# Weight sums, couples and last products in a two-layer encoder trunk: a change of order on one core

## The chip, the cores and the metric

The kernel runs on one core of a Trainium2 chip. The metric is the device time of one execution in microseconds (us). Engines are named as in the profile: PE is TensorE (PEld its weight loads), DVE is VectorE, ACT is ScalarE, POOL is GpSimd, SP is SyncE, which here only issues DMAs. A line number such as L233 is a line of the kernel before; in the changed kernel the same code stands one to three lines further down.

## The reference

Two layers over 256 tokens of width 2048, all in float32. Each layer is a token mixer and a gated MLP with a convolution of width 3 over the tokens, both with RMSNorm ahead and the residual added.

```python
h = x
for layer in range(DEPTH):                         # DEPTH = 2
    hn = rmsnorm(h, norm_mix_g[layer])
    mix = mlstm_mixer(...) if layer % 2 == 0 else hgrn_mixer(...)
    h = h + mix
    h = h + conv_glu(rmsnorm(h, norm_ffn_g[layer]), ffn_w_up[layer], ..., ffn_w_down[layer])
return rmsnorm(h, final_g)

def conv_glu(hn, w_up, conv_w, conv_b, w_down):    # D_FF = 5504
    a, v = jnp.split(hn @ w_up, 2, axis=-1)
    c = conv_b + sum(ap[:, j:j + s] * conv_w[j] for j in range(3))   # ap: a, padded by one token
    return (jax.nn.gelu(c, approximate=False) * v) @ w_down
```

The first mixer is a bidirectional mLSTM (8 heads), the second a bidirectional HGRN2 (16 heads); each is a projection of the normalized tokens, a recurrence by head, and an output projection.

## The kernel before

**Products.** A float32 product is made of three products of rounded halves: a weight tile `raw` is rounded by ACT to `wh` (L145), and DVE takes the rest, `wl` = `raw` - `wh` (L146). The tokens are split likewise. Every product is high times high, high times low and low times high.

**Stages.** The program runs, for each layer: the mixer with its projections; then the MLP in two parts, of 22 and 21 tiles of 128 of the hidden width. A part is an *up half* (a chunk of matmuls for each tile: L343 and L347, then the convolution, GELU and product, which give the token tiles `g`) and a *down stage* of two *pairs*, which add the part's share of `w_down` to the residual `hm`, each for two of the four blocks of 512 columns. `squares_by_seven` writes a pair's matmuls (L233).

**Couples.** A pair works through *units* of two tiles of the hidden width: unit 0 is tiles 0 and 1, and so on to unit 10 (in the second part a single tile). Over two tiles, two token halves and two column blocks, a plain unit needs 8 block products (24 matmuls). A *couple* is a unit done by 7 block products (21 matmuls) in the manner of Strassen and Winograd: for it the weights' sums T1 to T4 and the token tiles' sums S1 to S4 are needed. `SEVEN[part]` lists which units are couples. Four of the products gather in the PSUM tiles `mm`, the rest in `pc` (C11, C12, C21, C22: first index the token half, second the column block).

**Weight sums ahead of time.** T1 to T4 are made earlier and kept in device memory (`tscr`): `prepare` loads a couple's weights into `praw` (two DMAs on SP), makes four subtractions on DVE (L608) and stores the result (two DMAs on SP, L611). In a down stage the couple then loads them back: three quarters into a tile `T` (L196), one quarter into the end of `raw` (L197). `T` shares its three buffers with `avc`, the temporaries of the up chunks. A list of sums (`todo`) is worked off at a fixed pitch beside the matmuls, counted on the kernel's own clock (`side`, advanced by what the matmuls are taken to last); there are three lists in each layer: one in the mixer (`prepare_early(mp, layer, first, period)`: first load at `first`, a sum each `period`), one in each up half (period `(nf * 10.4 - 26.0) / len(todo)`, each load asked for one sum ahead; in the mixers a load comes half a period ahead of its sum). `shares` and `SPLIT` say how many of a pair's sums go to the mixer, to the first and to the second up half.

**Order.** Instructions are written down as the code meets them, and a scheduler then reorders each engine's list by its own estimates; `pin` (`tc.keep_in_program_order`) holds instructions in the written order. Each engine then works strictly in its list's order.

**The end.** The last pair does its units 8, 9 and 10 in `ending`: all products of token half 0, then those of half 1; after each half, `FinalNorm.half` (L495 to L508) adds the two blocks to `hm`, takes the mean square, scales by it and sends the rows out. L495 adds the first block of a half, L497 the second, L507 scales.

Of the kernel before, what the change touches and what calls it, by code (L numbers as in the profile page):

```python
# [46 lines left out]
LEAD = 48  # L47
TEMP = 3
GATES = 4 * AH
SEVEN = (1, 2, 3, 4, 6, 7, 8, 9), (1, 2, 3, 4, 5, 6, 7)  # L50
SPLIT = (0, 2, 5), (2, 2, 3)
END = 3
SCRATCH = 4096
SEVEN_MIX = (2, 4, 6)
# [9 lines left out]
def trunk_kernel(ctx, tc, xT, x_d, fg_d, pp_d, cst_d, w_gate, w_first, w_aq, w_ak, w_av, w_ao, w_aout, w_ao2,  # L64
                 w_bq, w_bv, w_bg, w_bout, w_bo2, w_up, w_d0, w_d1, w_d3, out, mscr, tscr):
    nc = tc.nc
    act, dve, pool, pe = nc.scalar, nc.vector, nc.gpsimd, nc.tensor
# [60 lines left out]
    pin = tc.keep_in_program_order  # L128
# [94 lines left out]
    def squares_by_seven(ch, fetch, ready):  # L223

        P1, P6, P7, P5 = psm_ = banks() + banks()
        C11, C12, C21, C22 = psa_ = [aux("pc") for _ in range(4)]
        begun = set()
        held.append(ch)

        def product(ps, x, w, stop):  # L230
            (xh, xl), (wh, wl) = x, w
            for i, (a, b) in enumerate(((xh, wh), (xh, wl), (xl, wh))):
                pe.matmul(ps, a, b, start=id(ps) not in begun, stop=stop and i == 2)  # L233
                begun.add(id(ps))

        def half(x, t):
            return x[:, t * P:(t + 1) * P], x[:, T + t * P:T + (t + 1) * P]

        def block(p, i):
            return tuple(w[:, i * 512:(i + 1) * 512] for w in p)  # L240

        def ending(u0):
            while len(ready) < ch.nk - 2 * u0:
                fetch()
            for t in range(2):
                c, left = (C11, C12, C21, C22)[2 * t:2 * t + 2], iter(ready)
                for k in range(2 * u0, ch.nk, 2):
                    p = next(left)[:2]
                    x0, end = half(ch.x(k), t), k + 2 >= ch.nk
                    product(c[0], x0, block(p, 0), end)  # L250
                    if k + 1 == ch.nk:
                        product(c[1], x0, block(p, 1), end)
                        break
                    q, x1 = next(left)[:2], half(ch.x(k + 1), t)
                    product(c[1], x1, block(p, 1), False)
                    product(c[0], x1, block(q, 0), end)
                    product(c[1], x0, block(q, 1), end)
                ch.half(c, t)

        units, last = (ch.nk + 1) // 2, max(ch.seven)  # L260
        for u in range(units):
            if ch.last and u == units - END:
                ending(u)
                held.pop()
                return
            fetch()
            p = ready.pop(0)
            end = u == units - 1
            if 2 * u + 1 == ch.nk:
                x = ch.x(2 * u)  # L270
                for ps, t, w in ((C11, 0, 0), (C12, 0, 1), (C21, 1, 0), (C22, 1, 1)):
                    product(ps, half(x, t), block(p[:2], w), True)
                side.tick(2.7)
                break
            x0, x1 = ch.x(2 * u), ch.x(2 * u + 1)
            A11, A21, A12, A22 = half(x0, 0), half(x0, 1), half(x1, 0), half(x1, 1)

            def products(*them):
                for ps, x, w in them:
                    product(ps, x, w, u == last and ps in psm_)  # L280
                    side.tick(0.65)

            def piece():
                fetch()
                q = ready.pop(0)[:2]
                return block(q, 0), block(q, 1)

            B11, B22 = block(p[:2], 0), block(p[:2], 1)
            if u in ch.seven:
                S1, S3, S2, S4 = ch.sums(u)  # L290
                products((P1, A11, B11), (C12, S4, B22))
                T2, T3 = piece()
                products((P6, S2, T2), (P7, S3, T3))
                B21, T1 = piece()
                products((C11, A12, B21), (P5, S1, T1))
                T4, _ = piece()
                products((C21, A22, T4))
                if u == last:
                    ch.mid(psm_)
                    ch.rest = ch.ends  # L300
                continue
            B21, B12 = piece()
            for ps, (x, w), (y, v) in ((C11, (A11, B11), (A12, B21)), (C12, (A11, B12), (A12, B22)),
                                       (C21, (A21, B11), (A22, B21)), (C22, (A21, B12), (A22, B22))):
                product(ps, x, w, False)
                product(ps, y, v, end)
                side.tick(1.3)
        held.pop()
        ch.done(psa_)
# [309 lines left out]
    def prepare_early(mp, layer, first, period):  # L619
        todo, finished = early[layer]  # L620
        side.push(prepare(lambda i: [mp.tile([P, 1024], F32, tag=f"p{j}", name="praw") for j in range(2)],
                          todo, first, period, finished, late, False))
# [42 lines left out]
    def mlstm(norm, nxt):  # L665
# [8 lines left out]
        box = {}  # L674
# [182 lines left out]
        chunks = []  # L857
        for pr in range(AH // 2):
# [36 lines left out]
            def done_first(ps, done_v=done_v):  # L895
                pq = aux("pq")
                for k in range(KT):
                    o = k % 4 * GATES
                    pin(pe.matmul(pq[o:o + GATES, 0:T], gw[:, k], hx[:, k], start=k < 4, stop=k >= KT - 4))
                gs = ev.tile([P, T], F32, tag="gs", name="gs")  # L900
                act.copy(gs, pq[:, 0:T])
                startup.close()
                begin()
                norm.finish()
                done_v(ps, note)
                side.push(start(gs))
                prepare_early(box["mp"], 0, 45.0, 19.0)

            last = {}

# [32 lines left out]
    def hgrn(norm, nxt):  # L943
        YT = [None] * KT
        stack = ExitStack()
        box = {}

        def begin():
            mp = box["mp"] = stack.enter_context(tc.tile_pool(name="hg", bufs=1))
            late(cst[:, C_LV:], cst_d[:, C_LV:])  # L950
            prepare_early(mp, 1, 30.0, 26.0)
            box["turn"] = 0
            lb = box["lb"] = mp.tile([P, KT], F32, name="lb")
            oml = box["oml"] = mp.tile([P, KT], F32, name="oml")
            t0 = mp.tile([P, 2, KT], F32, name="t0")
            t1 = mp.tile([P, KT], F32, name="t1")
            raw = pp[:, OFF["lb"]:OFF["lb"] + 2 * KT].rearrange("p (a b) -> p a b", a=2)
            dve.tensor_tensor(t1, raw[:, 0], raw[:, 1], ALU.max)
            for i in range(2):
                dve.tensor_tensor(t0[:, i], raw[:, i], t1, ALU.subtract)  # L960
            act.activation(t0, t0, AF.Exp)
            dve.tensor_tensor(t1, t0[:, 0], t0[:, 1], ALU.add)
            dve.reciprocal(t1, t1)
            for i in range(2):
                dve.tensor_tensor(t0[:, i], t0[:, i], t1, ALU.mult)
            dve.tensor_tensor(lb, t0[:, 0], t0[:, 1], ALU.add)
            dve.tensor_tensor(lb, lb, t0[:, 0], ALU.subtract)
            dve.tensor_scalar(oml, lb, -1.0, 1.0, ALU.mult, ALU.add)
# [137 lines left out]
        chunks, vs, gs, fs = [], [], [], []  # L1106
        for qd in range(BH // 4):
# [16 lines left out]
            for i in range(6):  # L1124
# [4 lines left out]
                n = 6 * qd + i  # L1129
# [3 lines left out]
        for n, ch in enumerate(fs):  # L1133
            if n in TMS:
                i = TMS.index(n)
# [11 lines left out]
    def ffn(layer, norm, nxt):  # L1147
        stack = ExitStack()
        ending = isinstance(nxt, FinalNorm)
        box = {}  # L1150
        chunks, pairs, lists = [], [], []
# [36 lines left out]
        for part, (f0, nf) in enumerate(((0, FA), (FA, FB))):  # L1188
            GT, SX, todo, finished = [], {}, [], []
# [13 lines left out]
            def two(src, c0, norm, seven, shares, GT=GT, SX=SX, nf=nf):  # L1203
                ch = pair(src, nf, c0, lambda k: GT[k], lambda u: SX[u], norm, seven)
                ch.waits, left = [], list(seven)
                for n, (todo, finished) in zip(shares, [early[layer]] + lists):
                    for u in left[:n]:
                        store(ch, src, u, todo)
                    if n:
                        ch.waits.append(finished)  # L1210
                    left = left[n:]
                assert not left
                pairs.append(ch)
                return ch

            w0, w1 = w_d0[layer][:, f0 * 1024:(f0 + nf) * 1024], w_d3[layer] if part else w_d1[layer]
            n = len(SEVEN[part])
            chunks.append(two(w0, 0, nxt if part else None, SEVEN[part], (0, 0, n) if part else (n, 0)))
            chunks.append(two(w1, 2, nxt if part and not ending else None, SEVEN[part], SPLIT[layer] if part else (0, n)))
            if part:  # L1220
                chunks[-1].last = ending
# [12 lines left out]
    for i in range(90):  # L1234
        o = i % 4 * QUAD
# [3 lines left out]
    chunks = mlstm(n0, n1)  # L1239
    c, close0 = ffn(0, n1, n2)  # L1240
    chunks += c
    c = hgrn(n2, n3)
    b = c[0].before
# [6 lines left out]
    c, close1 = ffn(1, n3, nf)  # L1250
# [102 lines left out]
```

## Time and profile before

| | |
|---|---|
| time, median of 3 runs | 2377.87 us (2377.03 to 2379.53) |
| profiled execution, its own time | 2380.58 us |
| its span, first to last instruction | 2378.3 us |
| busy PE, DVE, ACT, POOL | 99%, 83%, 61%, 9% of the span |
| DMA | 632.96 MB, mean 266 GB/s |
| weight sums loaded back (`T<-tscr`) | 63 |
| first mixer, MLP, second mixer, MLP | to about 390, 1090, 1675, 2378 us |

A row of the timeline gives the start in us from the span's start, the duration, the engine, the line, the operation, what is written and read, and how many were merged into the row; in brackets stands the idle time of the engine before it and what ended that. A row of the waits gives total, number and longest. A row of the windows gives the stretch and its length, then busy time and number of instructions for PE, PEld, DVE, ACT and POOL (or of one engine, if a line is picked out), the granted clock (1.00 is full), the share of the DMA engines and their GB/s.

### The profile page before, as it was taken

The numbers are of one execution on the slowest core, as the hardware profiler recorded it, in microseconds if no ns is written. First come the engines' busy times: TensorE is split into PE (matmuls) and PEld (weight loads), VectorE is DVE, ScalarE is ACT, GpSimd is POOL, SyncE is SP. The second block draws the span as 40 slices with busy tenths as digits, with TensorE's granted clock in tenths as the row PEclk, the third lists the DMA queues.
The fourth block names the chain that finished last, engine by engine and source line by source line (L and its number), as shares of the span: only waits on it lengthen the run. The fifth ranks groups of instructions, "written<-read, shape, count | busy, mean of one in ns | idle before, by whom it ended". The sixth has DMA issues, their size and how long they took to land.

```text
span 2378.3 us, 38347 instructions
## 1 busy us (share of the span) xinstructions
PE 2360.9 (99%) x14548; PEld 2019.2 (85%) x14548; DVE 1965.4 (83%) x3028; ACT 1459.1 (61%) x2321; POOL 203.9 (9%) x244
## 2 busy tenths in 40 slices
PE   9999999999999999999999999999999999999998
PEld 8888888888888888888888888888888888888886
DVE  7777687888888898887888878878788878888887
ACT  7655456555565555675777676776555566455565
POOL 0100000000000000000332322220000000000000
PEclk9999999999999999999999999999999999999999
DMA  8787655887898888986666666656778798888895
GB/s 300 240 273 266 229 186 198 301 284 266 280 345 289 308 282 291 362 295 230 244 219 245 227 225 229 218 172 232 265 263 282 273 329 306 296 272 287 287 357 188
DMA packets 121832, 632.96 MB, mean 266 GB/s; under 512 B 13728, under 2 KB 14240, under 8 KB 77232
## 3 DMA queue, kind: packets, MB, share of 16 engines
q1 hardware_dynamic: 119952, 626.51, 75.1%
q0 software_dynamic: 1120, 3.21, 0.8%
q8 instruction: 114, 1.87, 0.3%
q10 hardware_dynamic: 576, 0.79, 0.1%
q14 instruction: 70, 0.57, 0.1%
HBM read 562.24 MB, written 68.22 MB: 265 GB/s over the span
## 4 chain that ended last, share of the span: by engine, by line
PE 94%; DMA 3%; DVE 2%; issue 1%; ACT 0%; SPq 0%; POOL 0%; DVEq 0%; POOLq 0%; ACTq 0%
PE mm L343 36%; PE mm L347 18%; PE mm L359 16%; PE pc L233 13%; PE mm L233 7%; DMA T<-tscr 1%; DMA praw<-in_w_d 1%; DVE wl L146 1%; PE pn L822 1%; PE py L1080 1%; PE pd L1030 0%; PE pz L420 0%; PE pa L1030 0%; DMA Mb<-mscr 0%; ACT wh L145 0%
## 5 line engine op out<-in xcount | busy, mean ns | idle before, releaser
L343 PE MATMUL mm<-xt,wh 128*128 128x512 f32 x3776 | 1312.8, 394 | 0.7 <-issue 0.7
L146 DVE TENSOR_TENSOR wl<-raw,wh 128x1024 fp32r<-128x1024 f32 (+1 forms) x844 | 1035.9, 1233 | 267.1 <-ACT wh L145 257.3
L145 ACT CAST wh<-raw 128x1024 fp32r<-128x1024 f32 (+1 forms) x844 | 875.1, 1043 | 544.5 <-PE mm L343 326.9
L347 PE MATMUL mm<-xt,wl 128*128 128x256 f32 x3776 | 1043.4, 278 | 0.0
L343 PEld LDWEIGHTS mm<-xt,wh 128*128 128x128 f32 x3776 | 705.5, 188 | 161.1 <-issue 0.8
L347 PEld LDWEIGHTS mm<-xt,wl 128*128 128x128 f32 x3776 | 709.4, 188 | 5.2 <-issue 0.4
L359 PE MATMUL mm<-wh,xt 128*128 128x512 f32 x1024 | 322.8, 393 | 1.1 <-ACT xt L365 1.0
L233 PE MATMUL pc<-wh,g 128*128 128x512 f32 x776 | 262.8, 390 | 0.0
L359 PEld LDWEIGHTS mm<-wh,xt 128*128 128x128 f32 x1024 | 191.3, 188 | 40.6 <-ACT xt L365 1.4
L359 PE MATMUL mm<-wl,xt 128*128 128x512 f32 x512 | 198.1, 391 | 0.0
L608 DVE TENSOR_TENSOR praw<-praw 128x512 f32<-128x512 f32 x252 | 174.5, 692 | 26.4 <-DMA praw<-in_w_d 21.7
L233 PEld LDWEIGHTS pc<-wh,g 128*128 128x128 f32 x776 | 145.6, 188 | 30.2
L233 PE MATMUL pc<-wl,g 128*128 128x512 f32 x388 | 150.9, 389 | 0.0
L233 PE MATMUL mm<-wh,sx 128*128 128x512 f32 x396 | 141.6, 390 | 1.0 <-ACT wh L145 1.0
L146 DVE TENSOR_TENSOR wl<-T,wh 128x1024 fp32r<-128x1024 f32 (+1 forms) x132 | 125.8, 965 | 16.4 <-ACT wh L145 16.2
L145 ACT CAST wh<-T 128x1024 fp32r<-128x1024 f32 (+1 forms) x132 | 109.4, 835 | 46.4 <-PE pc L233 19.9
L567 POOL TENSOR_TENSOR hm<-hm,u 128x512 f32<-128x512 f32 x10 | 13.9, 1389 | 1225.5 <-DVE u L566 1225.5
L1167 ACT COPY avc<-mm 128x256 f32<-128x256 f32 x172 | 64.1, 373 | 79.3 <-PE mm L347 79.1
L1043 DVE TENSOR_TENSOR QK<-QK,G 128x256 f32<-128x256 f32 x224 | 106.8, 525 | 6.8 <-ACT kq L1022 6.2
L359 PEld LDWEIGHTS mm<-wl,xt 128*128 128x128 f32 x512 | 96.2, 188 | 18.7
L1022 ACT COPY kq<-QK 128x512 f32<-128x512 f32 x112 | 74.2, 668 | 46.0 <-DVE QK L1043 41.3
L233 PEld LDWEIGHTS mm<-wh,sx 128*128 128x128 f32 x396 | 74.2, 188 | 17.1 <-ACT wh L145 1.8
(237 smaller groups left out, 2225.0 us busy)
## 6 DMA issues: line engine op xcount, KB each, us to landing
raw<-in_w_up SPq DMA_DIRECT2D x172, 1024.0 KB, 5.5
tscr<-praw SPq DMA_DIRECT2D x126, 512.0 KB, 6.8
praw<-in_w_d SPq DMA_DIRECT2D x120, 512.0 KB, 6.6
raw<-in_w_bq SPq DMA_DIRECT2D x48, 1024.0 KB, 5.0
T<-tscr SPq DMA_DIRECT2D x63, 768.0 KB, 7.1
raw<-in_w_d SPq DMA_DIRECT2D x60, 768.0 KB, 6.2
raw<-in_w_ao SPq DMA_DIRECT2D x24, 1024.0 KB, 4.9
raw<-in_w_d SPq DMA_DIRECT2D x24, 1024.0 KB, 6.2
```

What stands on the lines that cost most here:

```text
L145: pin(act.copy(wh[:, :m], r))
L146: pin(dve.tensor_tensor(wl[:, :m], r, wh[:, :m].bitcast(F32), ALU.subtract))
L233: pe.matmul(ps, a, b, start=id(ps) not in begun, stop=stop and i == 2)
L343: pe.matmul(ps[f], wh[:, c:c + P], x, start=k + kk == 0, stop=False)
L347: pe.matmul(ps[f][:, 0:T], wl[:, c:c + P], x[:, 0:T], start=False, stop=k + kk == ch.nk - 1)
L359: pe.matmul(ps[t], x[:, a + t * P:a + (t + 1) * P], w[:, c], start=st and i == 0, stop=sp and i == 2)
L608: dve.tensor_tensor(out, x, y, ALU.subtract)
L822: pe.matmul(pn[:, 0:258], w, v, start=(i == 0), stop=(i == len(parts) - 1))
L1022: act.copy(m, blocks(QK, h))
L1043: dve.tensor_tensor(two[:, j], two[:, j], by[:, j], ALU.mult)
L1080: pe.matmul(py[:, c], AT[:, s if s == t else 2 + s], V[:, s, j * P:(j + 1) * P], start=(s == 0), stop=(s == 1))
L1167: act.copy(z, p[:, T:2 * T])
```

## The change

It changes four things. The last pair's 60 products are held in the written order, and those of token half 1 are written with all of column block 0 ahead of column block 1. In the first part of each MLP the couples stand at units 2 to 9 (before: 1 to 4 and 6 to 9). The first pair of that part takes six of its eight sums from the mixer and two from the first up half (before: all eight from the mixer); the second layer's last pair takes none from its mixer (before: two). So the mixers make 6 and 9 sums (before: 8 and 13), and each of the four up halves makes 12 (before: 10 and 12 in layer 0, 10 and 10 in layer 1). Lastly `prepare_early` starts the mixers' sums at 62 with a pitch of 25, and at 30 with a pitch of 38 (before: 45 and 19, 30 and 26). The count of couples, of sums (63) and of matmuls is the same.

```diff
-SEVEN = (1, 2, 3, 4, 6, 7, 8, 9), (1, 2, 3, 4, 5, 6, 7)
-SPLIT = (0, 2, 5), (2, 2, 3)
+SEVEN = (2, 3, 4, 5, 6, 7, 8, 9), (1, 2, 3, 4, 5, 6, 7)
+FIRST = 6
+SPLIT = (0, 2, 5), (0, 2, 5)
...
-        def product(ps, x, w, stop):
+        def product(ps, x, w, stop, pin=lambda ins: ins):
             (xh, xl), (wh, wl) = x, w
             for i, (a, b) in enumerate(((xh, wh), (xh, wl), (xl, wh))):
-                pe.matmul(ps, a, b, start=id(ps) not in begun, stop=stop and i == 2)
+                pin(pe.matmul(ps, a, b, start=id(ps) not in begun, stop=stop and i == 2))
...
             for t in range(2):
-                c, left = (C11, C12, C21, C22)[2 * t:2 * t + 2], iter(ready)
+                c, todo, left = (C11, C12, C21, C22)[2 * t:2 * t + 2], [], iter(ready)
                 for k in range(2 * u0, ch.nk, 2):
-                    p = next(left)[:2]
-                    x0, end = half(ch.x(k), t), k + 2 >= ch.nk
-                    product(c[0], x0, block(p, 0), end)
+                    p, x0 = next(left)[:2], half(ch.x(k), t)
+                    todo += [(0, x0, block(p, 0))]
                     if k + 1 == ch.nk:
-                        product(c[1], x0, block(p, 1), end)
+                        todo += [(1, x0, block(p, 1))]
                         break
                     q, x1 = next(left)[:2], half(ch.x(k + 1), t)
-                    product(c[1], x1, block(p, 1), False)
-                    product(c[0], x1, block(q, 0), end)
-                    product(c[1], x0, block(q, 1), end)
+                    todo += [(1, x1, block(p, 1)), (0, x1, block(q, 0)), (1, x0, block(q, 1))]
+                if t:
+                    todo.sort(key=lambda o: o[0])
+                end = [max(i for i, o in enumerate(todo) if o[0] == j) for j in range(2)]
+                for i, (j, x, w) in enumerate(todo):
+                    product(c[j], x, w, i == end[j], pin)
                 ch.half(c, t)
...
-                prepare_early(box["mp"], 0, 45.0, 19.0)
+                prepare_early(box["mp"], 0, 62.0, 25.0)
...
-            prepare_early(mp, 1, 30.0, 26.0)
+            prepare_early(mp, 1, 30.0, 38.0)
...
-            chunks.append(two(w0, 0, nxt if part else None, SEVEN[part], (0, 0, n) if part else (n, 0)))
+            chunks.append(two(w0, 0, nxt if part else None, SEVEN[part], (0, 0, n) if part else (FIRST, n - FIRST)))
```

What becomes of the order shows at three places.

**PE, the last products of the program.** `pc_23407` and `pc_23408` are the two column blocks of token half 0, `pc_23409` and `pc_23410` those of half 1; g16 to g20 are the token tiles. Before, the last rows but the very end:

```order
L233 MATMUL pc_23407<-wh_23762,g20_22952 128x512
L233 MATMUL pc_23408<-wh_23762,g20_22952 128x512
L233 MATMUL pc_23408<-wl_23763,g20_22952 128x512
L233 MATMUL pc_23408<-wh_23762,g20_22952 128x512
L233 MATMUL pc_23409<-wh_23756,g19_22843 128x512
L233 MATMUL pc_23409<-wl_23757,g19_22843 128x512
L233 MATMUL pc_23409<-wh_23756,g19_22843 128x512
L233 MATMUL pc_23410<-wh_23756,g18_22733 128x512
```

After these, 8 more rows follow there: two of `pc_23410`, three of `pc_23409`, three of `pc_23410`. The scheduler had mixed the halves: half 0 ends 12 matmuls before the end, and the two blocks of half 1 end three matmuls apart. Now:

```order
L234 MATMUL pc_23408<-wl_23763,g20_22952 128x512
L234 MATMUL pc_23408<-wh_23762,g20_22952 128x512
L234 MATMUL pc_23409<-wh_23717,g16_22513 128x512
L234 MATMUL pc_23409<-wl_23718,g16_22513 128x512
L234 MATMUL pc_23409<-wh_23717,g16_22513 128x512
L234 MATMUL pc_23409<-wh_23727,g17_22621 128x512
```

Half 0 ends 30 matmuls before the end; 15 of `pc_23409` follow, and then 15 of `pc_23410`.

**DVE, the first two heads of the first mixer.** `W`, `Wl`, `rd` and `y` belong to the heads, `praw` to the weight sums. Before:

```order
L608 TENSOR_TENSOR praw<-praw 128x512
L797 SCALAR_TENSOR_TENSOR W<-Mb,cc,cst 128x256
L797 SCALAR_TENSOR_TENSOR W<-Mb,cc,cst 128x128 x2
L797 SCALAR_TENSOR_TENSOR W<-Mb,cc,cst 128x256
L146 TENSOR_TENSOR wl<-raw,wh 128x1024
L825 TENSOR_TENSOR rd<-rd,emn 128x1
L608 TENSOR_TENSOR praw<-praw 128x512
L825 TENSOR_TENSOR rd<-rd,emn 128x1 x3
L826 RECIPROCAL rd<-rd 128x1
L608 TENSOR_TENSOR praw<-praw 128x512
```

And now, from the same place on:

```order
L800 SCALAR_TENSOR_TENSOR W<-Mb,cc,cst 128x256
L800 SCALAR_TENSOR_TENSOR W<-Mb,cc,cst 128x128 x2
L800 SCALAR_TENSOR_TENSOR W<-Mb,cc,cst 128x256
L147 TENSOR_TENSOR wl<-raw,wh 128x1024
L828 TENSOR_TENSOR rd<-rd,emn 128x1 x4
L829 RECIPROCAL rd<-rd 128x1 x4
L147 TENSOR_TENSOR wl<-raw,wh 128x1024
L833 SCALAR_TENSOR_TENSOR y<-pn,rd,y 128x256 x2
```

The first sum (L611 in the new numbering) now comes 18 rows later, behind the last `y` of the first two heads.

**SP, the start of the first down stage.** `raw<-in_w_d` of 128x2048 is a plain unit, of 128x1536 a couple; `T` and `raw<-tscr` are its stored sums. Before:

```order
L133 DMA raw<-in_w_d 128x2048
L611 DMA tscr<-praw 128x1024 x2
L133 DMA raw<-in_w_d 128x1536
L197 DMA raw<-tscr 128x512
L133 DMA raw<-in_w_d 128x1536
L196 DMA T<-tscr 128x1536
L197 DMA raw<-tscr 128x512
```

And now:

```order
L134 DMA raw<-in_w_d 128x2048 x2
L614 DMA tscr<-praw 128x1024 x2
L134 DMA raw<-in_w_d 128x1536
L198 DMA raw<-tscr 128x512
L134 DMA raw<-in_w_d 128x1536
L198 DMA raw<-tscr 128x512
L197 DMA T<-tscr 128x1536
```

Two plain units stand ahead of the first couple instead of one, so the first T is that of unit 2.

## The prediction

> **What bounds the kernel now.** I read the page first: the busy shares, then the chain that ended last.
>
> ```profile
> PE 2360.9 (99%) x14548; PEld 2019.2 (85%) x14548; DVE 1965.4 (83%) x3028; ACT 1459.1 (61%) x2321; POOL 203.9 (9%) x244
> PE 94%; DMA 3%; DVE 2%; issue 1%; ACT 0%; SPq 0%; POOL 0%; DVEq 0%; POOLq 0%; ACTq 0%
> ```
>
> TensorE is the bound, and the change leaves its work alone: the same 13,313 matmuls of the same shapes stand in both programs (eight couples by seven before and after, only at other units). So the change can only give back time in which PE stands still, or add such time. Who keeps PE waiting is in the view of waits:
>
> ```profile
> PE pd L1030 <- issue: 1.1, 1, 1.1
> PE mm L233 <- ACT wh L145: 1.0, 2, 0.6
> PE pz L1101 <- DVE y L1095: 0.8, 1, 0.8
> PE mm L343 <- issue: 0.7, 1, 0.7
> PE pn L822 <- DVE y L830: 0.7, 1, 0.7
> PE pc L233 <- DVE wl L146: 0.3, 1, 0.3
> ```
>
> That is 4.6 us in 2378, besides the start of the program. The other time without matmuls is the end, after the last of them. 0.2% of the median of 2377.87 us is 4.8 us, about what a measurement of this kernel can tell from no change; so nearly all of this would have to go for a gain that shows. A matmul's shown end runs past the next one's start (0.39 us each, every 0.227 us below), so I size stalls by starts.
>
> **The end.** The timeline of the last microseconds:
>
> ```profile
> 2354.17 8.84 PE pc L233 x39
> 2367.15 0.62 PE L233 MATMUL pc<-wh,g 128*128 128x512 f32 x2
> 2367.83 0.39 PE L233 MATMUL pc<-wh,g 128*128 128x512 f32 x1
> 2367.65 0.69 DVE L495 TENSOR_TENSOR hm<-hm,pc 128x512 f32<-128x512 f32 x1 [0.31 <-PE pc L233]
> 2368.25 1.41 DVE L507 SCALAR_TENSOR_TENSOR hm<-hm,fss,fg 128x512 f32<-128x512 f32 x2
> 2369.58 0.68 DVE L497 TENSOR_TENSOR hm<-hm,pc 128x512 f32<-128x512 f32 x1
> 2371.92 1.42 DVE L507 SCALAR_TENSOR_TENSOR hm<-hm,fss,fg 128x512 f32<-128x512 f32 x2 [0.67 <-POOL fss L502]
> ```
>
> PE is done at 2367.83 + 0.39 = 2368.22, but the add that needs the last block (L497) starts at 2369.58: DVE first scales the first token half (L507, twice), which the old order ended late. By the new order the first token half ends 30 matmuls before the end, 6.8 us at 0.227 (8.84/39), and the block of L495 15 matmuls, 3.4 us, before it. The first half's adds then start near 2361.4 and its scaling near 2364.5 (an add of 0.7 and then 2.34, as from L497 to the last L507 now), L495 near 2364.9; all DVE work but the last block's is over by about 2367. L497 then starts 0.11 us after PE's end, as L495 does now behind the matmul of 2367.15 (end 2367.54, start 2367.65): 2368.33. The rest (L497 to scaling, 2.34 us, and the output DMAs) stays: **1.25 us saved**. Less contention among the output DMAs could add some tenths.
>
> The held order has a price if weights come late: PE may no longer take another half's product. The 60 products start at about 2367.83 − 59 × 0.227 = 2354.4.
>
> ```profile
> 2353.71 1.23 DVE L146 TENSOR_TENSOR wl<-raw,wh 128x1024 fp32r<-128x1024 f32 x1 [0.67 <-ACT wh L145]
> 2356.64 2.35 DVE L146 TENSOR_TENSOR wl<-raw,wh 128x1024 fp32r<-128x1024 f32 x2
> ```
>
> The last three pieces are split by 2354.9, 2357.8 and 2359.0. The held order takes their low parts as products 13, 19 and 25 (counted from 0): at 2357.4, 2358.8 and 2360.1. So the cover is 0.9 us at its thinnest; if these pieces come 2 us later, PE loses 1.1 and most of the gain is gone. I count nothing.
>
> **Couples at units 2 to 9.** At the start of a down stage the first couples wait for their stored sums, whose tiles are those of the last up chunks:
>
> ```profile
> 637.50 0.39 PE L233 MATMUL pc<-wh,g 128*128 128x512 f32 x1
> 641.00 6.31 SPq L196 DMA_DIRECT2D T<-tscr  x3
> 647.60 1.05 ACT L145 CAST wh<-T 128x1024 fp32r<-128x1024 f32 x1 [1.93 <-DMA T<-tscr]
> 647.96 0.39 PE L233 MATMUL pc<-wh,g 128*128 128x512 f32 x1
> 648.70 0.73 PE L233 MATMUL mm<-wh,sx 128*128 128x512 f32 x2 [0.35 <-ACT wh L145]
> 1930.71 0.39 PE L233 MATMUL pc<-wh,g 128*128 128x512 f32 x1
> 1931.71 0.50 PE L233 MATMUL mm<-wh,sx 128*128 128x512 f32 x1 [0.62 <-ACT wh L145]
> ```
>
> Unit 0 (24 matmuls, 5.4 us) and unit 1 (21, 4.8 us) pass; then unit 2 waits for a sum that was asked for at 641.00. The stalls are 0.74 − 0.23 = 0.51 and 1.00 − 0.23 = 0.77 us. With units 0 and 1 plain, that second sum belongs to unit 3 and is needed at 637.5 + 2 × 5.4 + 4.8 = 653.1 or later, 4.5 us after its cast is through at 648.65. **1.25 us saved** in the two layers, between 0.5 (one of them stays, for tiles freed later) and 1.3. What is late next is nothing that I see: two plain units ask less of all engines.
>
> The cost is that couples now stand eight in a row. Each asks for a stored tile T of 768 KB and, by the code's shapes (128x1536 and 128x512), for 768 and 256 KB in `raw`: 1.835 MB in 21 × 0.227 = 4.77 us, 385 GB/s. The page's row of T, and windows inside such rows of couples:
>
> ```profile
> T<-tscr SPq DMA_DIRECT2D x63, 768.0 KB, 7.1
> 665.00:670.00 5.00, 5.00 (x24) 4.14 (x23) 3.24 (x4) 2.62 (x4) 0.00 (x0) 1.00 1.02 418
> 685.00:690.00 5.00, 5.00 (x24) 4.14 (x23) 5.00 (x7) 4.01 (x4) 0.00 (x0) 1.00 0.97 361
> 1010.00:1015.00 5.00, 5.00 (x24) 4.14 (x23) 4.32 (x5) 3.93 (x5) 0.00 (x0) 1.00 1.01 417
> ```
>
> In the windows the last column is GB/s, the one before it the DMA engines' share. The last lies late in a row of seven couples (units 1 to 7, 985 to 1018), at 417 and with PE full: the DMA keeps up. I take 0. [...]
>
> **Sums moved.** A sum is four subtractions on DVE (L608) and four DMAs on SP, two in and two out. The mixers lose two of eight and four of thirteen; the first up half of each layer goes from ten to twelve, as does the second of layer 1. The windows of L608 alone, then of all engines, for a half with ten sums, one with twelve, and the second mixer:
>
> ```profile
> 392.00:640.00 248.00, 27.35 (x40) 1.00 0.81 277
> 757.00:980.00 223.00, 32.88 (x48) 1.00 0.88 306
> 392.00:640.00 248.00, 248.00 (x1432) 216.85 (x1431) 209.07 (x337) 141.07 (x223) 0.70 (x1) 1.00 0.81 277
> 757.00:980.00 223.00, 223.00 (x1289) 194.95 (x1288) 195.71 (x312) 125.50 (x197) 0.00 (x0) 1.00 0.88 306
> 1100.00:1605.00 505.00, 502.24 (x4613) 431.84 (x4612) 412.30 (x687) 354.41 (x679) 143.35 (x176) 1.00 0.65 225
> ```
>
> Two more sums are 8 × 0.684 (27.35/40) = 5.5 us of DVE: 209 to 215 of 248, 87%. The half with twelve runs at 88%, with PE full for all 223 us. So the twelve **cost 0**, PE's matmuls hiding them; their DMAs on SP as well, beside the loads of `raw`.
>
> In the mixers a sum's load isn't asked for a sum ahead, so DVE, which works in order, waits at L608 and holds up what PE needs:
>
> ```profile
> DMA to landing us min/median/max: 2.6/6.6/10.1
> 86.26 0.69 DVE L608 TENSOR_TENSOR praw<-praw 128x512 f32<-128x512 f32 x1 [1.82 <-DMA praw<-in_w_d]
> 92.37 0.28 PE L822 MATMUL pn<-Vh,Wl 128*128 128x258 f32 x1
> 93.32 0.39 PE L822 MATMUL pn<-Vh,Wh 128*128 128x258 f32 x1 [0.67 <-DVE y L830]
> 1373.15 0.69 DVE L608 TENSOR_TENSOR praw<-praw 128x512 f32<-128x512 f32 x1 [2.21 <-DMA praw<-in_w_d]
> 1385.41 0.39 PE L359 MATMUL mm<-wh,xt 128*128 128x512 f32 x1
> 1386.63 0.66 PE L1101 MATMUL pz<-cst,y 128*128 128x128 f32 x2 [0.84 <-DVE y L1095]
> ```
>
> The first sum of the first mixer stood among the work of the first two heads; it now stands behind it, so 1.8 us of waiting and 4 × 0.68 of work leave DVE there, and the stall of 0.95 − 0.12 = **0.8 us** goes. In the second mixer the load has half the pitch to land, 19 of the kernel's own units rather than 13, so fewer of DVE's waits should last; but sums fall beside other heads. Of the 1.22 − 0.23 = 1.0 us there I count **half, 0.5**: between 0 (another head pays) and 1.0. New stalls of this kind: between 0 and one more of 1.0; I take 0.2, since one sum in thirteen made one.
>
> **The sum.** 1.25 + 1.25 + 0.8 + 0.5 − 0.2 = 3.6 us. The profiled execution took 2380.58 us (2.3 beyond its span of 2378.3), so its like would take 2377.0; that execution lies 2.7 above the median of the runs, so I put the gain there: 2377.87 − 3.6 = **2374.3 us**.
>
> **The rivals.**
> *All stalls go (faster).* The two waits on "issue" (1.1 and 0.7 in the table; by name nothing that the profile shows) may be tied to the mixers' load, and DVE there may be free enough for the whole 1.0: 3.6 + 0.5 + 0.2 + 1.8, with 0.3 at the output, is 6.4: 2371.5. For it: both lie in the second mixer, which loses four sums. Against: nothing names their cause, and the order of small matmuls there shifts anyway.
>
> *The mixers' waits only move.* The end and the couples give 2.5, but each mixer keeps a stall, one of 1.3 beyond now: 2376.7. For it: one slip in order anywhere in 500 us is enough, as at 1385. Against: fewer sums, longer leads.
>
> *The eight in a row starve (slower).* If the supply sits where the row of 685 has it, 361 GB/s at a share of 0.97, a couple needs 5.08 us, 0.31 more than PE; four rows of eight cost 10 us once the loaded-ahead tiles are used up, and 2384.3 results. It decides when the mean supply over a row falls below 385. [...] Against: seven in a row at 417, without a stall.
>
> *Not what it says:* the order might not hold at the end; it is written as held, so I see no room for this.
>
> **How the numbers follow.** Forecast 0.44 (own range 2373.2 to 2375.6), waits moved 0.20, all go 0.28, starving 0.08. Faster by over 0.2% (below 2373.1) is the third alone, 0.28; slower by over 0.2% (above 2382.6) the fourth, 0.08; within, 0.64. The range of 8 in 10 takes in the forecast, the moved waits and most of the faster case, and stops short of starving: 2370.8 to 2378.0.
>
> **What would show it.** Right: L497's counterpart starts within 0.2 us of PE's last end; no wait of `mm` on `wh` in the first units of a down stage; the stall at 92 gone; PE full in all four up halves. Wrong: idle PE before `pc` in the last 14 us (weights late in the held order), waits of ACT on DMA late in units 5 to 9, new waits of PE on `y` or `W` in the mixers, or a wait on `praw` that stops PE in an up half.

## The result, and the profile after

| | before | after |
|---|---|---|
| median in the same comparison | 2379.54 us (2377.03 to 2381.53, 10 runs) | 2371.99 us (2370.0 to 2376.66, 10 runs) |
| ratio | | 0.9973, 95% interval 0.9963 to 0.9982 |
| profiled execution, its span | 2380.58, 2378.3 us | 2372.06, 2370.1 us |

Faster by 0.27%, some 6.4 us by that ratio (the medians lie 7.55 us apart). The forecast was 2374.3, with 3.6 us saved; the measured time lies inside the range, but beyond the forecast's own band (2373.2 to 2375.6) and close to the rival by which all stalls go (2371.5). The page of the changed kernel, its busy times:

```profile
PE 2357.5 (99%) x14548; PEld 2019.1 (85%) x14548; DVE 1965.9 (83%) x3028; ACT 1464.1 (62%) x2321; POOL 196.9 (8%) x244
T<-tscr SPq DMA_DIRECT2D x63, 768.0 KB, 8.1
```

The work is the same: as many instructions on PE, DVE and ACT. The waits, PE's rows but that of its first instruction, and the two of DVE on the loads of sums:

```profile
PE mm L346 <- issue: 1.5, 1, 1.5
PE mm L362 <- ACT xt L368: 0.6, 1, 0.6
PE pc L234 <- DVE wl L147: 0.4, 1, 0.4
...
DVE praw L611 <- DMA praw<-in_w_d: 26.0, 18, 3.5
DVE praw L611 <- issue: 17.1, 14, 2.2
```

PE's 4.6 us of waits have become 1.9; the row on `xt` lies at 9.7, in the start, which the 4.6 leave out (it is 1.0 there before). Those on `wh`, on `y` (both mixers) and on `pd` are gone; the longest left is one on "issue", at a place that had none before. DVE waits longer for `praw` (before: 21.7 us on the DMA), and the span is 8.2 us shorter all the same.

**By stage.** The following table is worked out from the trace: I cut the program where PE has done the same number of matmuls and compare the stages' lengths, by the matmuls' starts. The first row is the profiled execution of before; the others are differences to it (us). "End" is from PE's last start to the span's end. Stages that are left out differ by 0.03 at most (in e10 by 0.13), and the start of the program varies (-1.4 to +1.9, in one run +4.4). A row is one execution and need not be the typical one: those of e2 and e9 are the fastest of their kernels' runs, those of e1, e3 and e7 the slowest.

```
                       mixer 1  down 0a  up 0b  mixer 2  down 1a  up 1b  last down    end    span
before                  362.59   122.54 219.90   495.62   120.17 222.90     104.50  10.50  2378.3
after                    -1.97    -0.65   0.00    -2.83    -1.29   0.00       0.11  -1.33  2370.1
after, once more         -2.17    -0.65   0.00    -4.39    -1.29   0.00       4.23  -1.33  2371.5
e1  end alone             0.43     0.57   0.00     0.21    -1.29   0.00       0.00  -1.33  2376.8
e2  couples alone        -0.06    -0.65   0.00    -0.93    -1.29   0.00       0.03  -0.02  2374.1
e3  sums alone           -2.04    -0.49   0.00    -2.33     0.15   0.00       0.98  -0.21  2376.2
e4  old start and pitch  -0.37    -0.65   0.00    -2.28    -1.29   0.00       1.07  -1.31  2373.2
e5  sorted, not held     -1.75    -0.65   0.00    -2.27    -1.29   0.00       0.61  -0.35  2371.2
e6  held, not sorted     -1.93    -0.65   0.00    -2.79    -1.29   0.00       0.00  -1.19  2370.0
e7  122 for 90           -2.09    -0.65   0.00    -2.81    -1.29   0.00       1.84  -1.32  2376.4
e8  sums from 62 on      -1.93     0.61   0.00     1.30     0.25   0.00       0.30  -0.01  2377.6
e9  half ends 10 early   -2.09    -0.65   2.48    -3.15    -1.29   3.25       0.03  -1.33  2374.3
e10 loads asked earlier   5.59     0.12   0.00     1.57    -0.83   0.00       0.30  -0.01  2384.1
e12 74 for 90            -2.07    -0.65   0.00    -3.15    -1.29   0.00       0.31  -1.32  2370.0
```

Down 0a and 1a are the first parts' down stages, with the moved couples; up 0b and 1b the second up halves. After: 0.26 at the start, 1.97, 0.65, 2.83 and 1.29, less 0.11, and 1.33 are the 8.2 us of span.

**The end**, on the timeline after; its counterpart is the first one shown of before:

```profile
2358.03 0.69 DVE L498 TENSOR_TENSOR hm<-hm,pc 128x512 f32<-128x512 f32 x1 [1.02 <-PE pc L234]
2358.63 1.41 DVE L510 SCALAR_TENSOR_TENSOR hm<-hm,fss,fg 128x512 f32<-128x512 f32 x2
...
2360.93 0.39 PE L234 MATMUL pc<-wh,g 128*128 128x512 f32 x1
2361.36 0.69 DVE L500 TENSOR_TENSOR hm<-hm,pc 128x512 f32<-128x512 f32 x1 [1.19 <-PE pc L234]
2363.70 1.41 DVE L510 SCALAR_TENSOR_TENSOR hm<-hm,fss,fg 128x512 f32<-128x512 f32 x2 [0.67 <-POOL fss L505]
```

The add of the last block (L500, before L497) follows PE's last end, 2361.32, by 0.04 us; before, by 1.36. DVE has scaled the first half before that and waits 1.19 us for PE. No piece of weights came late in the held order.

**Mixer 1**, DVE around the heads' `y` and its first sum, and **down 0a**, ACT at the first couples:

```profile
89.42 0.87 DVE L833 SCALAR_TENSOR_TENSOR y<-pn,rd,y 128x256 f32<-128x256 f32 x2
...
99.84 1.42 DVE L611 TENSOR_TENSOR praw<-praw 128x512 f32<-128x512 f32 x2 [2.19 <-DMA praw<-in_w_d]
...
640.51 1.57 ACT L146 CAST wh<-T 128x1024 fp32r<-128x1024 f32 x2 [1.80 <-DMA T<-tscr]
646.65 1.05 ACT L146 CAST wh<-T 128x1024 fp32r<-128x1024 f32 x1
```

The first sum still waits for its load (2.19 us; before 1.82), but at 99.8, behind the heads' `y`. ACT still waits for the first `T`, but that is now unit 2's, which PE needs only when two units are done.

**The up halves**, all with twelve sums, and a row of couples in down 0a (columns as before):

```profile
390.00:635.00 245.00, 245.00 (x1419) 214.28 (x1418) 210.75 (x343) 140.41 (x220) 0.70 (x1) 1.00 0.84 292
2024.00:2256.00 232.00, 232.00 (x1341) 202.90 (x1341) 200.04 (x316) 128.39 (x199) 5.11 (x6) 1.00 0.86 302
665.00:670.00 5.00, 5.00 (x24) 4.14 (x23) 4.34 (x5) 3.93 (x5) 0.00 (x0) 1.00 1.02 403
685.00:690.00 5.00, 5.00 (x24) 4.14 (x23) 5.00 (x8) 2.78 (x3) 0.00 (x0) 1.00 1.00 385
```

PE is full in both, and in the windows of the two other halves too (760 to 980 and 1680 to 1918). The eight couples in a row run at 385 to 403 GB/s, which is what they need by the prediction's sum.

### The profile page after: what moved, and what is told of

Read it like the earlier page. It is cut to its first block, busy times and chain, and to the rows that moved or that the text cites. A ratio compares the mean times of both kernels' runs of the same rounds, so it can differ in the third digit from the quotient of the medians.

```text
span 2370.1 us, 38326 instructions
## 1 busy us (share of the span) xinstructions
PE 2357.5 (99%) x14548; PEld 2019.1 (85%) x14548; DVE 1965.9 (83%) x3028; ACT 1464.1 (62%) x2321; POOL 196.9 (8%) x244
## 3 DMA queue, kind: packets, MB, share of 16 engines
q8 instruction: 114, 1.87, 0.3%
## 5 line engine op out<-in xcount | busy, mean ns | idle before, releaser
L611 DVE TENSOR_TENSOR praw<-praw 128x512 f32<-128x512 f32 x252 | 174.8, 694 | 43.7 <-DMA praw<-in_w_d 26.0
```

The source lines that it names most:

```text
L611: dve.tensor_tensor(out, x, y, ALU.subtract)
```

## The experiments

The theory was the prediction's: four independent pieces. The rivals to each: that a part's gain comes from another part, or is chance. The first four kernels share one comparison (before 2380.32 us, 32 runs).

**e1, the end alone.** Before, with the `product` and `ending` of the change (held and sorted), nothing else.

> The kernel before with the held and sorted end alone. Theory (the pieces add up, each with its own place): PE's last product ends as before within the scatter of the earlier stages, at most 0.2 us of new idle PE in the last 14 us; the last add starts within 0.2 us of PE's end instead of 1.36 us; time 1.3 us less than before (-0.05%). Rival (the held order lets PE run ahead or behind in the last stage): PE's time from the first product of the last pair to its end changes by over 0.5 us.

2378.09 us, ratio 0.9992 (0.9983 to 1.0001), which does not exclude no change; the stage shows it: the end gave 1.33, as in after, and no weights came late. The other differences, in stages that this edit leaves alone, show what the same code differs by from run to run; its waits in the mixers are those of before:

```profile
PE pn L824 <- DVE y L832: 0.7, 1, 0.7
PE pz L1103 <- DVE y L1097: 1.5, 1, 1.5
PE mm L233 <- ACT wh L145: 0.8, 1, 0.8
PE pd L1032 <- issue: 1.1, 1, 1.1
```

**e2, the couples alone.**

```diff
-SEVEN = (1, 2, 3, 4, 6, 7, 8, 9), (1, 2, 3, 4, 5, 6, 7)
+SEVEN = (2, 3, 4, 5, 6, 7, 8, 9), (1, 2, 3, 4, 5, 6, 7)
```

> The kernel before with couples at units 2 to 9 alone. Theory: the wait of PE at the third unit of both first down stages goes, and the first pairs of layers 0 and 1 are 0.65 and 1.3 us shorter as in the changed kernel; time 1.9 us less than before (-0.08%). As predicted, by starts of the two stalls alone: 1.25 us less. Rival (eight in a row starve): ACT waits on DMA late in units 5 to 9 and PE with it, no gain or a loss of up to 10 us.

2377.73 us, ratio 0.9992 (0.9983 to 1.0). Down 0a gave 0.65 and down 1a 1.29, to 0.01 the same in all runs that have these couples. With the old couples both vary: they stand above that floor by 0.65, 1.22, 0.16, 1.26 and 0.77 (before, e1, e3, e8, e10) and by 1.29, 0, 1.44, 1.54 and 0.46. So the move brings the two stages to a floor that was missed by 1.8 us on average. Nothing starved.

**e3, the sums alone.** Before, with the new `SPLIT`, `FIRST`, the shares of the first pair and both `prepare_early` lines.

> The kernel before with the new shares of sums and the new starts and pitches in the mixers alone (couples still at units 1 to 4 and 6 to 9, end as before). Theory (sums in the mixers hold up DVE, and DVE the heads): first mixer 1.9 us shorter, second 2.8 us shorter, up halves unchanged; time 4.8 us less than before (-0.2%). Rival (the gain in the second mixer is a chance of the order there, above all of PE's waits on nothing shown, 2.2 us in all before): first mixer 1.9 us shorter, second anywhere between 2 longer and 3 shorter, with the change in those waits on issue.

2374.11 us, ratio 0.9978 (0.9969 to 0.9987). This part is the largest: 2.04 in mixer 1 and 2.33 in mixer 2, and it costs 0.98 in the last down stage.

**e4, which half of that part?** The change, but with the old first times and pitches.

```diff
-                prepare_early(box["mp"], 0, 62.0, 25.0)
+                prepare_early(box["mp"], 0, 45.0, 19.0)
-            prepare_early(mp, 1, 30.0, 38.0)
+            prepare_early(mp, 1, 30.0, 26.0)
```

> The changed kernel with the old starts and pitches in the mixers (45 and 19, 30 and 26), so as few sums but as early and with as short a lead as before. Theory (place and lead of the sums count): the first sum stands among the first two heads again and the first mixer loses its 1.9 us; the second, with waits of DVE on praw again, loses about 1; time 2.9 us over the changed kernel. Rival (the count alone matters): time within 1 us of the changed kernel.

2376.53 us, ratio 0.9982 (0.9973 to 0.9991). The waits on `y` are back in both mixers, though these have only 6 and 9 sums:

```profile
PE pn L825 <- DVE y L833: 0.7, 1, 0.7
PE pz L1104 <- DVE y L1098: 0.6, 1, 0.6
```

Mixer 1 keeps 0.37 of 1.97. So it is when the sums come and how long ahead they are loaded, not how many there are, that takes these waits away; for mixer 1 the next run tells the two apart, for mixer 2 none does. In mixer 2 the whole yet came out 2.28 shorter, since no wait on "issue" fell into this run (below).

**e8, the start of mixer 1's sums alone.** Before, with one number changed: the first load is asked for at 62, so all eight sums come 17 of the kernel's units later, at the old pitch of 19.

> The kernel before with one number changed: the first mixer's sums begin at 62 instead of 45, eight of them at the old pitch of 19. Theory (the place of the first sum among the first two heads makes the 2 us there): the first mixer is 1.6 to 2.0 us shorter than before. Rival (the lead or the count of sums): at most 0.5 us shorter.

2379.57 us, a single time. Mixer 1 gave 1.93 of after's 1.97: starting the sums later is the whole gain there, with as many of them and as short a lead as before. Mixer 2, whose code is untouched, was 1.30 longer than before: that stage varies by about 1 us either way (0.21, -0.93 and 1.30 in e1, e2 and e8). The differences lie at the waits already named: by the starts, the one on `y` cost 0.5 to 0.7 more than in the execution of before in all three, and those on "issue" came and went.

**e5 and e6, the end's two halves.** Both from the change. e5 sorts the second half but lets the scheduler reorder; e6 holds the written order without sorting.

```diff
e5:
-                    product(c[j], x, w, i == end[j], pin)
+                    product(c[j], x, w, i == end[j])
e6:
-                if t:
-                    todo.sort(key=lambda o: o[0])
```

> The changed kernel with the last products sorted but not held. Theory (it is the held order that lets token half 0 end early; the sort alone is undone by the scheduler, which mixes the halves again): the last add starts over 0.8 us after PE's end and the time from PE's last start to the end of the span is 10.2 to 10.5 us, as before, instead of 9.2. Rival (the sort does it): 9.2 us.

> The changed kernel with the last products held in order but not sorted by column block in token half 1. Theory: token half 0 ends 30 products early as in the changed kernel, so DVE is free at PE's end; but the add of the first block of half 1 comes only three products, 0.7 us, before that of the second, so its square and mean fall behind it: 0 to 0.7 us of the 1.3 are lost, 9.2 to 9.9 us from PE's last start to the end. Rival (the early column block is what counts): 10.2 us or more.

2373.21 and 2372.13 us, a single time each. The end was 10.15 us in e5 and 9.31 in e6 (10.50 before, 9.17 after). The last adds of e5, then of e6:

```profile
2361.10 0.39 PE L234 MATMUL pc<-wh,g 128*128 128x512 f32 x1
2361.17 1.40 DVE L510 SCALAR_TENSOR_TENSOR hm<-hm,fss,fg 128x512 f32<-128x512 f32 x2
2362.49 0.68 DVE L500 TENSOR_TENSOR hm<-hm,pc 128x512 f32<-128x512 f32 x1
```

```profile
2360.44 0.69 DVE L496 TENSOR_TENSOR hm<-hm,pc 128x512 f32<-128x512 f32 x1 [1.52 <-PE pc L234]
2360.69 0.39 PE L234 MATMUL pc<-wh,g 128*128 128x512 f32 x1
2361.12 0.69 DVE L498 TENSOR_TENSOR hm<-hm,pc 128x512 f32<-128x512 f32 x1
```

In e5 the first half's scaling still stands ahead of the last add; in e6 only the add of the other block does, back to back. Holding the halves apart gives 1.19 of the 1.33 without the sort; the sort alone gives 0.35, and 0.14 on top of the held order.

**e7 and e12, the waits on "issue".** The change, with another count in the loop that keeps PE busy at the program's start; each pass shows as two matmuls in the trace (180 for 90), so this shifts all later matmuls of PE, each with its weight load, by 64 or 32 places against the fetches of 16 KB in the last section, and changes nothing else behind the start.

```diff
-    for i in range(90):
+    for i in range(122):      # e7; 74 in e12
```

> The changed kernel with 122 instead of 90 idle products at the start, which shifts all later PE instructions by 64 places (a matmul and its weight load each) and costs 0 to 0.8 us there. Theory (PE's waits on issue in the second mixer come from fetching its instructions in blocks of 256, seen as queue 8 in the page, and so hang on where a block ends): the wait of 1.6 us at 1226 goes or moves to another place of the mixer. Rival (they hang on the work there): a wait of 1.2 to 1.7 us at the same matmul. The last down stage stays within 0.2 us of the changed kernel's, or 1 us longer, as in two of the runs with this distribution of sums.

> The changed kernel with 74 instead of 90 idle products at the start, which shifts all later PE instructions back by 32 places. Theory (blocks of instructions): the wait on issue in the second mixer is not at the matmul of 1226 any more: it moves or goes, and no wait on issue stands in the start. Rival: a wait of 1.2 to 1.7 us at the same matmul.

e7: 2376.33 us, ratio 0.9987 (0.9977 to 0.9996) to a before of 2379.16; the start of its profiled execution is 4.42 us longer, where I expected 0.8 at most. In it lie the wait of 3.3 below and, from 8.0 to 14.6, a stretch with the granted clock at 0.50. e12: 2372.0 us, a single time. The wait of after at 1226 moved in both, to 1244 and to 1507. Waits of e7, then of e12:

```profile
PE idle L1239 <- issue: 3.3, 1, 3.3
PE mm L362 <- issue: 1.2, 1, 1.2
```

```profile
PE pd L1033 <- issue: 0.7, 1, 0.7
```

Of the seven executions with fewer sums in the mixers and the old count, five have the wait at that place (1226 to 1230), and two (e4 and the repeat) have none. So the place in PE's stream seems to count, and not the data; with one execution each of e7 and e12, how much is chance is not shown.

**e11, the change once more,** the same program.

> The changed kernel once more, beside the one above. All theories: 0.9963 to 0.9982 of the kernel before; first mixer 1.9 us and second 2.3 to 2.8 us shorter than before, both first down stages at 121.9 and 118.9 us, last down stage 104.5 to 106.3, 9.2 us from PE's last start to the end; the wait on issue near 1226 again.

2372.78 us (before 2378.62), ratio 0.9974 (0.9963 to 0.9984), as the first time. Its profiled execution had no wait on "issue" in mixer 2, which was 4.39 shorter than before, and lost 4.23 in the last down stage; the prediction's sign of no wait of `mm` on `wh` in the first units of a down stage fails here. Its rows there, SP, ACT and PE:

```profile
2243.98 0.40 SPq L614 DMA_DIRECT2D tscr<-praw  x1
2244.43 0.51 SPq L197 DMA_DIRECT2D T<-tscr  x1
...
2256.87 1.05 ACT L146 CAST wh<-T 128x1024 fp32r<-128x1024 f32 x1 [4.31 <-DMA T<-tscr]
2264.73 1.03 ACT L146 CAST wh<-raw 128x1024 fp32r<-128x1024 f32 x1
2265.81 0.50 PE L234 MATMUL mm<-wh,g 128*128 128x512 f32 x1 [1.75 <-ACT wh L146]
```

and the counterparts in the trace of before, whose last down stage starts 9.7 us later:

```profile
2239.31 2.40 SPq L611 DMA_DIRECT2D tscr<-praw  x2
...
2250.03 0.42 SPq L196 DMA_DIRECT2D T<-tscr  x1
```

With twelve sums the last store stands directly ahead of the first load of a stored `T` on SP, 0.45 us apart by their starts; before, the row of the last stores ends 8.3 us ahead of it. After's row of that load is at 2244.20, nearly the time of the repeat's, although PE was 2.7 us further on in the repeat: the load is asked for when the last sum is done, and not when PE comes near the couple. Measured against PE's progress (the row's time less the sum of the stages' differences), with the loss in the last down stage:

```
first T asked for later than before, us   last down, us
0.0 to 0.6  (e1, e2, e8, e10: ten sums)    0.00  0.03  0.30  0.30
0.5 to 1.5  (e6, e5, after, e3, e4)        0.00  0.61  0.11  0.98  1.07
1.7 to 3.2  (e12, e7)                      0.31  1.84
4.1         (after, once more)             4.23
```

**e9, the sums of the up halves earlier,** to take this loss away. The change with a shorter pitch, so that a half's last sum is made 10 of the kernel's own units sooner.

```diff
-(nf * 10.4 - 26.0) / len(todo)
+(nf * 10.4 - 36.0) / len(todo)
```

> The changed kernel with the pitch of the sums in all four up halves worked out with 36 in place of 26, so that the last sum of a half is stored some 10 us earlier. Theory (with twelve sums the last stores of the last up half hold up SP's queue, so that T and raw of the last down stage's first couple come late; this costs 0 to 1.8 us there, 0.6 in the mean of five runs): the last down stage is 104.5 us in all looks, no wait of PE in its first 15 us; time 0.6 us less than the changed kernel run beside it, at most within the scatter. Rival (the waits there come from the loads of the final weights or from chance): 0 to 1.8 us as before.

2379.88 us against 2378.62 of before, ratio 1.0005 (0.9996 to 1.0014): worse than the change by all that it gave. The loss in the last down stage did go, as expected (0.03, the first `T` asked for as early as before), but the time did not follow. The second up halves, full in every other run, lost 2.48 and 3.25 in the profiled execution, which is the fastest of the eleven (2376.3 us), so the median lost more than these show:

```profile
PE mm L350 <- DVE wl L147: 3.4, 3, 1.6
...
905.76 0.69 DVE L611 TENSOR_TENSOR praw<-praw 128x512 f32<-128x512 f32 x1 [4.10 <-DMA praw<-in_w_d]
```

DVE waits 4.1 us for a sum's load, and the `wl` behind it in its order comes late for PE. At twelve sums these halves are thus near what they hide: a pitch that is shorter by some 5% already shows.

**e10, a longer lead for the mixers' loads** at the old times of the sums, in before: if DVE's waits for `praw` make PE's waits on `y`, they should go.

```diff
-            yield period / 2
+            yield period / 2 if ahead else period * 3 / 4
-            yield period / 3
+            yield period / 3 if ahead else period / 12
-                prepare_early(box["mp"], 0, 45.0, 19.0)
+                prepare_early(box["mp"], 0, 40.25, 19.0)
-            prepare_early(mp, 1, 30.0, 26.0)
+            prepare_early(mp, 1, 23.5, 26.0)
```

> The kernel before with sums in the mixers at the same times, but each load asked for three quarters of the pitch ahead of its sum instead of half of it. Theory (in the second mixer DVE stands at L608 for late loads, which then keeps PE from y): DVE's waits for praw fall from 9.1 us to under 4 in the second mixer, and PE's wait at pz near 1385 goes: second mixer 1.2 us shorter, besides up to 1 us either way from waits on issue. Rival (the work of the sums itself, not their waiting, delays y): the wait at pz stays at 0.8 to 1.5 us. In the first mixer the sums stand even earlier, so no gain there.

2386.1 us, a single time. My expectation failed: the mixers became 5.59 and 1.57 longer, and DVE's waits in the second grew (before: 9.1 us on the DMA). Waits from 1100 to 1605; PE's longest of the whole span, which lies in the first mixer, and the window behind it; and DVE's first sum there:

```profile
DVE praw L608 <- DMA praw<-in_w_d: 8.6, 4, 4.2
DVE praw L608 <- DMA praw<-in_w_bo: 5.0, 2, 3.1
```

```profile
PE pz L850 <- DVE y L845: 2.6, 1, 2.6
...
110.60:114.00 3.40, 3.22 (x11) 2.83 (x12) 2.82 (x6) 3.40 (x7) 1.59 (x1) 0.50 0.79 257
...
77.08 0.69 DVE L608 TENSOR_TENSOR praw<-praw 128x512 f32<-128x512 f32 x1 [4.30 <-DMA praw<-in_w_d]
```

The scheduler also set the first sums higher in DVE's list (the first starts at 77.1 us, before at 86.3): it waits 4.30 us for its load all the same, and the heads' work stands behind it. After PE's wait of 2.6 us the granted clock was 0.50 for 3.4 us, which added about 0.9 to the 5.59 (an estimate: 3.40 less the row's 11 matmuls at the 0.227 from start to start of 128x512). The lead by itself was therefore not tested; that the place in DVE's order counts again fits this, but one run with both changed does not show it.

## Why the prediction was right, and where it was not

- **The end, 1.25 us: right** in size (1.33) and way: L500 right behind PE's last end, and the cover for late weights held. The tenths from the output DMAs did not come: from the last scaling's start to the end of the span it was 6.4 us before (2371.92 to 2378.3) and after (2363.70 to 2370.1).
- **Couples, 1.25: way right, size too small.** The step read the stalls of one execution (0.51 and 0.77). Stage by stage the gain was 0.65 and 1.29: the second stage also lost smaller amounts, which no row of the waits names. In other runs of the old order these stages lose from nothing to 1.5 us each. One trace gave one draw of it.
- **Mixer 1, 0.8: way right, size too small.** The step priced the one stall at 92. Between 88 and 96 us the gain was 1.44, as `pn` had also been held up at 91 (0.29 us) and in smaller bits; the wait on `Wl` at 82, 0.32 before, is still 0.25. Another 0.42 came from 107 to 130, where PE waits in neither kernel (last section). e8 shows that starting the sums later gives 1.93 in all.
- **Mixer 2, 0.5 - 0.2: the step that failed most.** It measured 2.83, and 2.3 to 4.4 in the runs of the new sums. By the starts of PE's matmuls the wait on `y` with its two followers was 1.43, not 1.0, and all of it went, where I counted half; with the old pitch (e4) just 0.2 of it went, so the longer pitch did it, by the place or by the lead. The waits on "issue" at 1407 and 1458 (together 2.19 by starts) came back as one of 1.63 at 1226; in the repeat none came, and 1.43 + 2.19 is 3.6 of the 4.39. The rival that tied these waits to the mixers' load is not settled. Against it, they seem to move with PE's instruction count (e7, e12) and differ between runs of one program. For it, in the five executions with the old number of sums each of the two places had a wait four times (1407: 1.1 to 1.4 us; 1458: 0.2 to 0.7), and in the seven with fewer sums and the same count never. The rest, 0.8 us in small pieces, is not settled either; it was 0.8 in after and in the repeat alike, so it is hardly chance.
- **Twelve sums, 0: right where I looked, wrong behind it.** Up 0b and 1b are equal to 0.01 us. But I named only PE's matmuls and the loads of `raw` as what stands beside the DMAs, and did not ask what is queued on SP behind the last store: the next stage's first `T`. That cost 0 to 4.2 us in the last down stage, 1.1 in the mean of the eight executions with twelve sums at the new kernel's pitch.
- **Eight couples in a row, 0: right.** The rows at 403 and 385 GB/s have PE full, as the prediction judged from the row at 417.

So the sign and the places were right, and the pieces in the mixers were too small, as I summed named stalls over 0.3 us and not the stages' lost time. The likeliest case, within 0.2% of before, is not what came: 0.27% is just outside, though its interval (0.18 to 0.37%) takes in 0.2. The gain was nearly twice the forecast one; that the time still lies inside the range is owed to the range's width, and the near hit on the rival of 2371.5 is in part luck: the kernel before was 1.7 us slower in this comparison than the median from which the forecast starts, and that rival had both waits on "issue" gone, while in the profiled execution one of 1.5 came instead.

## What to carry to other kernels

Price a removed stall from the length of its whole stage, by the starts of the bound engine's instructions, and by more than one execution: the waits' table showed about half of what these stages had to give back. Background work on DVE cost more by its place here than by its amount (mixer 1 was 1.93 us shorter with all eight sums later in e8, and 0.37 with six at the old times in e4); put it behind the work that the bound engine waits for. When such work is moved to where it seems free, look one stage further, at what stands behind its last store in the same queue (here 0 to 4.2 us).

## What the runs showed of the hardware

**PE's waits on "issue" end soon after an instruction fetch begins.** By a fetch is meant a transfer of 16 KB on queue q8, which carries nothing else and whose kind the page gives as "instruction": 114 of them in each kernel (1.87 MB), for 29,096 records of PE, so one for some 256 on the whole. After's wait, on PE's timeline:

```profile
1226.17 0.28 PE L350 MATMUL mm<-xt,wl 128*128 128x256 f32 x1
1227.91 0.50 PE L346 MATMUL mm<-xt,wh 128*128 128x512 f32 x1 [1.46 <-issue]
```

The fetch ahead of it began at 1225.49 and took 0.94 us; 539 of PE's records (matmuls and weight loads) lie between its begin and that of the fetch before. PE went on 2.4 us after the begin. Before's wait at 1457.9 has 513 records between (fetch at 1455.94, on at 1458.92); before's at 1407 comes with a fetch begun at 1406.01, and PE goes on at 1408.42, again 2.4 us. All 17 waits on "issue" in these traces end 2.2 to 3.0 us after the begin of such a fetch. In the repeat, 494 lie between at the place of 1226, and PE did not wait. In e1, e2 and e4 522 to 525 lie there, and no wait shows either, so this count alone does not tell where PE waits. The waits in the second mixer were 0.2 to 1.5 us, none to three in an execution. Why PE waits at some fetches and not at others stays open.

The wait at 1407 is of another kind: only 167 records lie between its fetch and the one before, but PE stands in a row of short matmuls.

```profile
1406.49 0.82 PE L1030 MATMUL pd<-kq 128*32 128x32 f32 x72
1408.42 0.26 PE L1030 MATMUL pd<-kq 128*32 128x32 f32 x6 [1.11 <-issue]
```

PE's last 256 records ahead of that wait took 2.28 us (1.35, 1.96 and 1.73 ahead of those of e7 at 1244, e12 at 1507 and e10 at 1414), less than the 2.4 from the begin of a fetch until PE goes on: here PE was through 256 records in less time than that.

**The granted clock was 0.50 behind three of PE's waits:** from 8.0 to 14.6 us in e7 (wait of 3.3), from 11.1 to 14.5 in e3 (1.8, in the start) and from 110.6 to 114.0 in e10 (2.6; with the estimate above, some 0.9 us more than the wait's length). Waits of up to 1.75 us later in the program left it at 1.00 (e11).

**A stage with the same instructions varies by 1 us** (mixer 2 in e1, e2 and e8), and a down stage that begins with couples by up to 1.5, while the up halves and projections, in which PE hardly waits, repeat to 0.03 but for e9 and e10. One difference has no wait behind it: 120 matmuls of the first mixer, from about 108 us on, took 21.08 us in before, e1, e2 and e4 and 20.69 in the nine executions whose sums begin at 62, with the granted clock at 1.00 in each. The cause is open.
